# Two hybrid blocks on one core: the row-tiled matmuls of three mixers put on the full 128-row array

## The chip, the cores and the metric

The kernel runs on one core of one Trainium2 chip. TensorE (PE, with its weight loads listed as PEld), VectorE (DVE), ScalarE (ACT), GpSimd (POOL) and the DMA queue of SyncE (SP) work side by side. The metric is the device time of one execution in microseconds (us), as the median of the runs of a kernel.

## The reference

The reference is a first block and a second block on 512 grid tokens of 1024 features (the first block also reads 256 context tokens). Three places matter here.

The first block's mixer has an mLSTM with four heads, keys and queries 64 wide, values 128 wide. Per chunk, and in both directions of time, the output adds what the chunk's own scores give and what the carried state gives:

```
qk  = einsum('bhtd,bhsd->bhts', qb, kb) * w
num = einsum('bhts,bhse->bhte', qk, vb) + inter_w[..., None] * einsum('bhtd,bhde->bhte', qb, c_mem)
den = sum(qk, axis=-1) + inter_w * einsum('bhtd,bhd->bht', qb, n_mem)
h_out = num / maximum(abs(den), exp(-m_t))[..., None]
```

The second block has sparse attention: 16 heads of 64 in two groups, with three branches. A query of the selected branch sees its four best blocks of 64 keys, of the window branch its own window; both are masked softmaxes over scores q k^T. The second block also has a state-space mixer (32 heads of 64, chunks of 128), in which a decay `exp(acum[t] - acum[s])` of each head multiplies the scores of its group.

## The kernel before, in words

Activations lie feature-major, 128 features on the partitions and tokens along the free axis. Projections are done in three passes of fp32r matmuls over a high part and a low part of both operands (`mm3`, L210 to L212; L552 to L554 token-major). A matmul of fp32 operands shows as two instructions in the trace, one of fp32r as one.

A matmul whose operands lie on all 128 partitions uses the whole array; the profile writes it as 128*128 (rows*columns). One whose operands lie on 64 or 8 partitions is issued to a tile of 64 or 32 rows, written 64*128 or 8*128; one that writes 64 output partitions to a tile of 64 columns, 128*64.

The order of the work on every engine is set by a scheduler that plays the program on a timeline of its own (`schedule_with_timeline_sim=True`), led by priorities in program order; `later(n)` lets a piece yield. So a change of one instruction can move others. PSUM has eight banks, by use: `pa`, `pb` and `pf`; sparse attention has three banks of each of `pa` and `pb`, and two of `pf`.

The places that are touched:

- **mLSTM** (`ml_scan`). `iw` holds the query weights. L791 spreads them, L794 multiplies them into `qs` (4 multiplies of 128x512). Then, for each of four heads, L804 makes scores, L811 spreads maxima, L815 to L821 make the weights `wt` on DVE and ACT, and for each of four chunks and two directions L826 multiplies the weights with the values (128 rows) and L827 adds the queries times the carried state `cst`, 64 rows: the partitions of that head. Projections of the output gate (L552 to L554) fill gaps.
- **Sparse attention** (`nsa_step`). There are 64 steps: eight pairs of heads, four chunks `c` of queries, two heads of a pair. Each makes the scores of two branches `b` over `n = (c+1)*128` keys in a `pb` bank: L1399 takes the queries `q` (the head's high part on its own 64 partitions and its low part on the other 64) times the high part of the keys `kh`, which stands on both halves; L1400 adds the high part of the queries times the low part of the keys `kl`, 64 rows; for b = 0 and c of 2 or 3, L1402 adds the selection (`selT` times `cselr`, 8 rows); L1403 adds the causal mask on the last 128 columns. DVE takes the maximum (L1404), ACT the exponentials (L1406), which frees the bank; PE then transposes the weights (L1424) and multiplies them with the values (L1444, 128*64). Projections of z, in bank `pf`, fill gaps.
- **State-space mixer** (`ssd_group`). L1731 spreads a head's running decay over 128 partitions (`selr` times `acr`, 64 rows: 32 heads' high and low parts), L1751 does it for two heads at a time with `prs`.

```
nc.tensor.matmul(ps[:, :n], q[:, cc], kh[:, :n], start=True, stop=False)
nc.tensor.matmul(ps[:, :n], q[rows, cc], kl[rows, :n], start=False, stop=False)
if b == 0 and c >= 2:
    nc.tensor.matmul(ps[:, :n], E["selT"][g][:, c - 2, :], E["cselr"][:, :n], start=False, stop=False)
nc.tensor.matmul(ps[:, c * 128:n], E["idr"], E["cmr"], start=False, stop=True)
```

Of the kernel before, what the change touches and what calls it, by code (L numbers as in the profile page):

```python
# [10 lines left out]
F32 = mybir.dt.float32  # L11
F32R = mybir.dt.float32r
# [4 lines left out]
OP = mybir.AluOpType  # L17
AX = mybir.AxisListType
PSUM = bass.MemoryType.PSUM
# [21 lines left out]
class Kern:  # L41
# [6 lines left out]
    def banks(self, stage):  # L48
        """the eight banks of PSUM, by use, from here on"""
        pa, pb, pf = PS[stage]  # L50
        assert pa + pb + pf == 8
        if PS[max(stage - 1, 0)] == PS[stage] and stage:
            return
        self.psx.close()
        self.ps = self.psx.enter_context(self.tc.tile_pool(name="ps", bufs=1, space=PSUM, reuse_waits="tile"))
        self.psb = {"pa": pa, "pb": pb, "pf": pf}
# [13 lines left out]
    @contextmanager  # L70
    def later(self, n):
        """what is issued here yields to the next n instructions"""
        p = self.tc.cur_priority
        self.tc.cur_priority = p + n
        yield
        self.tc.cur_priority -= n
# [13 lines left out]
    def tmpf(self, name="tmpf"):  # L90
        """for work that fills gaps: not in line with the rest"""
# [28 lines left out]
    def lower_bounds(self, l0, l1, vec):  # L120
        """softmax over two rows of logits, first entry (columns [128, 8])"""
# [12 lines left out]
        # log(1 - lb)  # L134
# [4 lines left out]
    def columns(self, name, items, tag="pa"):  # L139
        """items: (key, ap of n*128 contiguous values, n); gives columns [128, n] of each."""  # L140
# [19 lines left out]
    def to_T(self, dst, src, ntok):  # L160
        """src DRAM [ntok,1024] -> dst [128, 8, ntok]"""
# [36 lines left out]
    def cols(self, w, c0, n):  # L198
        """columns c0..c0+n of w [K, N] as [128, K/128, n]"""
# [3 lines left out]
    def wrows(self, w, r0, nb):  # L203
        """row blocks r0.. (128 each) of w [K, N] as [128, nb, N]"""
# [9 lines left out]
    mvp = None      # pool of the rows' own room  # L214
# [4 lines left out]
    def silu_cols(self, aps, name):  # L219
        """columns of silu(c): [128, 8, len(aps)]"""  # L220
# [30 lines left out]
    def matvec(self, dst, w, sc, n, c0, nb, bias, tag=None):  # L251
        """dst [128, nb, n] = columns c0.. (nb blocks of 128) of silu(c) @ w + bias (bias [128, nb])"""
# [31 lines left out]
    def sumsq(self, x, n, tag, w2=None):  # L284
        """sums over the features of x^2 and, if asked for, of w2 x^2 [128 (all rows the same), n] in PSUM; x [128, 8, n]"""
# [20 lines left out]
    def table(self, name):  # L306
        """the activation table that comes next, after what has been issued"""
# [12 lines left out]
    def rstd(self, p, n, dim, name="rstd", dst=None, both=False, then=None):  # L320
        """1/sqrt(p/dim + eps) from PSUM p [128, n]; both: with the table that has both functions; then: the next table"""
# [7 lines left out]
    def halves(self, x, A, B):  # L329
        """the parts of norm_split for the grid's tokens, by half"""  # L330
        return [(x[:, :, t:t + 256], 256, A, B, t) for t in (0, 256)]

    def stats(self, parts):
        """1/rms of each of parts [(x, n, ..)]"""
# [4 lines left out]
    def norm_split(self, batches, hi, lo, rs=None):  # L339
        """batches: [[(x, n, A, B, t0)]]: hi + lo[:, :, t0:t0 + n] = x * rstd * A + B"""  # L340
# [21 lines left out]
    def ffn(self, w1, w2, hi, lo, segs, ends, begin=None, fill=()):  # L362
        """segs: [(t0, n, x, gate)]: x += gate * swiglu(hi + lo); gate already holds the half.
        ends: the segments for the first and last products, smaller for what waits and comes next"""
# [58 lines left out]
def constants():  # L423
# [29 lines left out]
    k["k_csel"] = (np.arange(512)[None, :] // 64 == np.arange(8)[:, None]).astype(f)  # L453
# [24 lines left out]
FB = (1, 1, 2)     # matrix-vector products beside a head of the mLSTM, of the HGRN, beside its last head  # L478
# [8 lines left out]
class Mix1:  # L487
    """HGRN2 and mLSTM over the context (256 tokens) and the grid (512 tokens)."""

    def mix1(self, i, hi, lo, vec, mrg, early):  # L490
        """hi, lo: [128, 8, 768] (grid tokens 0..511, context 512..767); mrg: DRAM [8, 128, 512]"""
# [36 lines left out]
    # one 128-column block, feature-major: fn(psum [128, n], t0, n)  # L528
# [11 lines left out]
    # token-major, 256 columns: fn(psum [128, 256], chunk)  # L540
# [16 lines left out]
    def wtok(self, w, c0):  # L557
        """256 columns of w, as two halves over k"""
# [10 lines left out]
    # ---------------------------------------------------------------- mLSTM  # L569
    def ml_project(self, i, w, vec):  # L570
# [10 lines left out]
        # q (chunks 0, 1: grid only) and k (chunks 2, 3), padded for the convolutions  # L581
# [3 lines left out]
        for ch in (2, 3, 0, 1):  # L585
# [15 lines left out]
            if ch == 3:  # L601
                # by half of the grid: the second one's norm comes later
# [8 lines left out]
        # v, token-major, with a column of ones  # L611
# [40 lines left out]
    def ml_scan(self, i, w, vec):  # L652
        nc, ml = self.nc, self.ml
        R = 56                                   # rows (dir, chunk, head): 0..23 forward, 32..55 backward
        # token-major gates, then rows
# [14 lines left out]
        row = lambda n: ml.tile([128, 128], F32, name=n)[:R]  # L670
        I, F = pr_[:R, 0:128], row("F")
        nc.vector.tensor_copy(F, pr_[:R, 128:256])
        # log sigmoid(f) = min(f, 0) - log1p(exp(-|f|))
# [8 lines left out]
        # cumulative sums and maxima within the chunks  # L682
# [6 lines left out]
        # the maximum carried from chunk to chunk  # L689
# [7 lines left out]
        ch = ml.tile([1, 4, 64], F32, name="ch")     # sum, maximum, carried m, carry weight  # L697
# [14 lines left out]
        mm = ml.tile([128, 2], F32, name="mmc")[:R]  # carried m, last maximum  # L712
# [5 lines left out]
        cwp = ml.tile([128, 2, 16], F32, name="cwp")  # [dir, (chunk, pair)]  # L718
# [3 lines left out]
        sw, iw, mt = (row(n) for n in ("sw", "iw", "mt"))  # L722
# [13 lines left out]
        # states  # L736
# [13 lines left out]
        for c in (4, 5, 0, 1, 2, 3):  # L750
# [13 lines left out]
            if c == 5:  # L764
                # context states -> first grid chunk of each direction
# [17 lines left out]
        # queries scaled for the states  # L783
        qs = ml.tile([128, 4, L], F32, name="qs")
        for pr in range(2):
            for d in range(2):
# [7 lines left out]
                nc.vector.tensor_mul(qs[:, pr * 2 + d, :], self.qT[:, pr, :], p)  # L794
        # scores, outputs
        self.hml = ml.tile([128, 4, 4, 128], F32, name="hml")
        ss = ml.tile([128, 4, 4], F32, name="mss")
        for h in range(4):
# [22 lines left out]
            for c in range(4):  # L821
                po = self.pt("pb")
                for d in range(2):
# [3 lines left out]
                    nc.tensor.matmul(o, qs[rows, pd, c * 128:(c + 1) * 128], cst[rows, pd, c, :], start=False, stop=True)  # L827
# [38 lines left out]
    # ---------------------------------------------------------------- HGRN2  # L866
# [8 lines left out]
    def hg_front(self, i, w, vec, h):  # L875
        """the projections of a head and what follows from them alone"""
# [12 lines left out]
        # of each direction: the sums of the log decays, B, and A = B + log k (backward) or B - log k (forward)  # L889
# [3 lines left out]
        for d in range(2):  # L893
# [32 lines left out]
            # the keys themselves, both directions added  # L926
# [9 lines left out]
    def hg_back(self, vec, h, mrg, front):  # L936
# [3 lines left out]
        # pairs at every level  # L940
# [6 lines left out]
        for d in range(2):  # L947
            B, A, Tt = BA[:, 1 + d, :L], BA[:, 3 * d, :L], Ta[:, d, :8]
            X, Y = BA[:, 2 * d, :L], BA[:, 2 * d + 1, :L]   # what the first and the second halves take
            sq, sk = (1, 0) if d == 0 else (0, 1)      # which half holds the queries / the keys  # L950
# [46 lines left out]
            # states between the chunks  # L997
# [3 lines left out]
            # U: from the chunk's start, V: to its end; queries and keys or keys and queries  # L1001
# [20 lines left out]
            # context  # L1022
# [15 lines left out]
            # transposed keys  # L1038
# [24 lines left out]
        # scores of both directions in one [key, query] tile  # L1063
# [19 lines left out]
        # norm over the head, gate  # L1083
# [11 lines left out]
        else:  # L1095
            # nothing reads the grid's rows any more
# [22 lines left out]
class Mix2:  # L1119
    LAT = [(0, 512)]  # L1120

    # ------------------------------------------------------------- rope tables
    def rope_tables(self, i, pool, cosd, sind):
        """cos and sin of the positions' angles, [128, 512], to DRAM"""
# [1417 lines left out]
```

## Time and profile before

| what | value |
|---|---|
| median of 3 runs | 2950.13 us (2944.2 to 2953.55) |
| span of the profiled execution | 2933.2 us |
| median less that span | 16.9 us |
| instructions | 41489 |
| PE busy | 2799.7 us, 95% (16545 matmuls) |
| PEld busy | 2114.3 us, 72% |
| DVE busy | 1548.8 us, 53% |
| ACT busy | 1000.1 us, 34% |
| POOL busy | 257.3 us, 9% |
| DMA | 373.95 MB, 40% of 16 engines' span |

The span is the time from the first to the last instruction of the profiled execution; the execution's own device time is not listed apart from the runs, so what lies around the span is taken as the 16.9 us between it and the median (11.0 to 20.4 us with the lowest and highest run). Times in a timeline count from the start of the span. A matmul's duration includes its pipeline, so two matmuls in a row overlap in the list; the time that one costs is the distance from its start to the next start.

### The profile page before, as it was taken

To read this page: it belongs to the slowest core of one execution; us is meant where nothing else is said; L and a number is where in the kernel's file an instruction comes from. 1 tells how busy PE (TensorE), PEld (TensorE's weight loads), DVE (VectorE), ACT (ScalarE), POOL (GpSimd) and SP (SyncE) were. 2 spreads that over 40 slices of the span, in tenths; PEclk is the share of its full clock that TensorE was granted. 3 is DMA by queue.
4 is the path that set the end of the run, shared out by engine and by line. 5 is a ranking of instruction groups with operands and counts; after the bars stand their busy time and mean duration, and the time that the engine had idled before them with its cause. 6 is when DMAs were issued, how large, how long until landed. Compare 5 with 4: busy or idle time off the path is not lost. (4 is left out here: it accounts for less than half of the span.)

```text
span 2933.2 us, 41489 instructions
## 1 busy us (share of the span) xinstructions
PE 2799.7 (95%) x16545; PEld 2114.3 (72%) x16546; DVE 1548.8 (53%) x3002; ACT 1000.1 (34%) x1793; POOL 257.3 (9%) x301
## 2 busy tenths in 40 slices
PE   7999999999998889999998999999999999989997
PEld 5788888889786666688887777666777768855553
DVE  6333333357358995543436556655666654543334
ACT  5211112144236663322224334444444533311112
POOL 2000000002001211000001000111222120000000
PEclk9999999999999899999999999999999999999999
DMA  7422122142512348533334332101233466378885
GB/s 259 139 87 79 51 65 65 59 129 72 151 52 65 85 155 284 170 94 98 95 90 142 95 92 74 30 12 45 80 101 104 131 204 203 110 272 280 289 305 186
DMA packets 386997, 373.95 MB, mean 127 GB/s; under 512 B 20321, under 2 KB 316645, under 8 KB 386546
## 3 DMA queue, kind: packets, MB, share of 16 engines
q1 hardware_dynamic: 386802, 371.28, 40.3%
q8 instruction: 131, 2.15, 0.3%
q14 instruction: 64, 0.52, 0.1%
HBM read 343.70 MB, written 27.53 MB: 127 GB/s over the span
## 5 line engine op out<-in xcount | busy, mean ns | idle before, releaser
L191 ACT CAST whi<-wraw 128x1024 fp32r<-128x1024 f32 x277 | 285.8, 1042 | 758.9 <-PE pppa L211 340.0
L210 PE MATMUL pppa<-lath,whi 128*128 128x512 f32 (+4 forms) x1344 | 521.9, 389 | 15.0 <-ACT whi L191 6.0
L211 PE MATMUL pppa<-latl,whi 128*128 128x512 f32 (+3 forms) x1344 | 519.9, 387 | 4.7 <-DVE latl L358 3.5
L212 PE MATMUL pppa<-lath,wlo 128*128 128x512 f32 (+3 forms) x1344 | 515.2, 385 | 0.5 <-DVE wlo L192 0.5
L192 DVE TENSOR_TENSOR wlo<-wraw,whi 128x1024 fp32r<-128x1024 f32 (+1 forms) x273 | 330.8, 1218 | 255.0 <-ACT whi L191 245.5
L210 PEld LDWEIGHTS pppa<-lath,whi 128*128 128x128 f32 (+3 forms) x1344 | 252.5, 188 | 81.1 <-ACT whi L191 12.9
L211 PEld LDWEIGHTS pppa<-latl,whi 128*128 128x128 f32 (+2 forms) x1344 | 252.2, 188 | 67.6 <-DVE latl L358 5.0
L212 PEld LDWEIGHTS pppa<-lath,wlo 128*128 128x128 f32 (+2 forms) x1344 | 252.1, 188 | 58.3 <-issue 4.5
L211 PE MATMUL pppb<-hl,whi 128*128 128x512 f32 (+1 forms) x576 | 195.4, 341 | 0.0
L210 PE MATMUL pppb<-hh,whi 128*128 128x512 f32 (+1 forms) x576 | 193.1, 344 | 0.0
L212 PE MATMUL pppb<-hh,wlo 128*128 128x512 f32 (+1 forms) x576 | 191.6, 341 | 0.0
L416 DVE SCALAR_TENSOR_TENSOR xT<-pppb,sG,xT 128x512 f32<-128x512 f32 (+1 forms) x144 | 96.8, 690 | 135.0 <-PE pppb L212 134.8
L396 DVE TENSOR_TENSOR hf<-sg,pppa 128x256 f32<-128x256 f32 (+1 forms) x68 | 39.7, 584 | 232.5 <-PE pppa L212 232.0
L210 PE MATMUL pppf<-lath,whi 128*128 128x512 f32 x320 | 129.7, 405 | 7.9 <-ACT lath L1823 2.9
L2109 PE MATMUL pppa<-ew,xg 128*64 128x512 f32 x512 | 131.2, 597 | 0.0
L210 PE MATMUL pppa<-ctxh,whi 128*128 128x256 f32 (+1 forms) x440 | 124.1, 282 | 5.4 <-DVE W L912 5.1
L212 PE MATMUL pppf<-lath,wlo 128*128 128x512 f32 x320 | 127.8, 400 | 0.6 <-DVE wlo L192 0.6
L211 PE MATMUL pppf<-latl,whi 128*128 128x512 f32 x320 | 128.0, 400 | 0.0
L210 PEld LDWEIGHTS pppb<-hh,whi 128*128 128x128 f32 x576 | 108.0, 188 | 27.3 <-issue 5.8
L212 PE MATMUL pppa<-ctxh,wlo 128*128 128x256 f32 (+1 forms) x440 | 124.2, 282 | 0.0
L211 PE MATMUL pppa<-ctxl,whi 128*128 128x256 f32 (+1 forms) x440 | 123.8, 281 | 0.3 <-POOL ctxl L356 0.3
L211 PEld LDWEIGHTS pppb<-hl,whi 128*128 128x128 f32 x576 | 108.4, 188 | 16.1 <-issue 3.4
(698 smaller groups left out, 5195.5 us busy)
## 6 DMA issues: line engine op xcount, KB each, us to landing
wraw<-in_ffn_w_dram SPq DMA_DIRECT2D x132, 512.0 KB, 4.0
wraw<-in_w_in_dram SPq DMA_DIRECT2D x102, 512.0 KB, 4.2
ew<-in_w_exp_gate_dram SPq DMA_DIRECT2D x64, 512.0 KB, 9.6
ew<-in_w_exp_up_dram SPq DMA_DIRECT2D x64, 512.0 KB, 8.7
ew<-in_w_exp_down_dram SPq DMA_DIRECT2D x32, 1024.0 KB, 11.2
mraw<-in_w_mod_dram SPq DMA_DIRECT2D x40, 512.0 KB, 7.0
wraw<-in_w_mod_dram SPq DMA_DIRECT2D x32, 512.0 KB, 4.3
mraw<-in_w_ada_dram SPq DMA_DIRECT2D x32, 512.0 KB, 7.0
```

The source lines that it names most:

```text
L191: nc.scalar.copy(hi[:, :n], raw[:, :n])
L192: (nc.gpsimd if pool else nc.vector).tensor_sub(lo[:, :n], raw[:, :n], hi[:, :n].bitcast(F32))
L210: nc.tensor.matmul(out, wh, xh, start=start, stop=False)
L211: nc.tensor.matmul(out, wh, xl, start=False, stop=False)
L212: nc.tensor.matmul(out, wl, xh, start=False, stop=stop)
L396: nc.vector.tensor_mul(h[:, :n], sg[:, :n], pp[1])
L416: nc.vector.scalar_tensor_tensor(x[:, o, :], p[:, :n], gate[:, o:o + 1], x[:, o, :], op0=OP.mult, op1=OP.add)
L2109: nc.tensor.matmul(ph[x * 64:x * 64 + 64, :], xg[:, k, pr * 128 + x * 64:pr * 128 + x * 64 + 64], wts[k // 4 * 2 + x][:, k % 4, :], start= ...
```

## The change

L827, L1400, L1402, L1731 and L1751 are issued over all 128 rows; L791, L804 and L811 (64 and 56 rows) stay as they are:

- mLSTM: `qs` gets a second axis for the two heads of a pair. The half of the partitions that is the other head's is zeroed by two memsets on POOL, and L794's four multiplies of 128 partitions become eight of 64. The state matmul then reads all of `qs` and `cst`. To make room, `sw`, `iw` and `mt` take the buffers of `e`, `w1` and `dd`.
- Sparse attention: the low-part matmul reads all 128 partitions of `q` and `kl`. Both halves of `kl` are already the same, so the low part of the queries times the low part of the keys is added as well. `selT` and `cselr` become 128 rows; the constant is 128x512 with zero rows, `selT` is zeroed on DVE before its first 8 rows are written, once for each of two groups.
- State-space mixer: `selr`, `prs` and `acr` become 128 rows; the lower 64 of `acr` are zeroed once on DVE.

```diff
-    k["k_csel"] = (np.arange(512)[None, :] // 64 == np.arange(8)[:, None]).astype(f)
+    cs = np.zeros((128, 512), f)
+    cs[:8] = np.arange(512)[None, :] // 64 == np.arange(8)[:, None]
+    k["k_csel"] = cs
...
-        sw, iw, mt = (row(n) for n in ("sw", "iw", "mt"))
+        sw, iw, mt = (row(n, tag) for n, tag in (("sw", "e"), ("iw", "w1"), ("mt", "dd")))
...
-        qs = ml.tile([128, 4, L], F32, name="qs")
+        qs = ml.tile([128, 4, 2, L], F32, name="qs")
+        for q in range(2):
+            nc.gpsimd.memset(qs[64 - q * 64:128 - q * 64, :, q, :], 0.0)
...
-                nc.vector.tensor_mul(qs[:, pr * 2 + d, :], self.qT[:, pr, :], p)
+                for q in range(2):
+                    r = slice(q * 64, q * 64 + 64)
+                    nc.vector.tensor_mul(qs[r, pr * 2 + d, q, :], self.qT[r, pr, :], p[r, :])
...
-                    nc.tensor.matmul(o, qs[rows, pd, c * 128:(c + 1) * 128], cst[rows, pd, c, :], start=False, stop=True)
+                    nc.tensor.matmul(o, qs[:, pd, h % 2, c * 128:(c + 1) * 128], cst[:, pd, c, :], start=False, stop=True)
...
-            cselr = na.tile([8, 512], F32R, name="cselr")
+            cselr = na.tile([128, 512], F32R, name="cselr")
             t = self.tmp("csel")
-            nc.sync.dma_start(t[:8, :], i["k_csel"])
-            nc.vector.tensor_copy(cselr, t[:8, :])
+            nc.sync.dma_start(t, i["k_csel"])
+            nc.vector.tensor_copy(cselr, t)
...
+                nc.vector.tensor_scalar(selT, self.ident[:, None, :].to_broadcast([128, 2, 128]), 0.0, None, op0=OP.mult)
...
-            nc.tensor.matmul(ps[:, :n], q[rows, cc], kl[rows, :n], start=False, stop=False)
+            nc.tensor.matmul(ps[:, :n], q[:, cc], kl[:, :n], start=False, stop=False)
...
-            acr = sd.tile([64, L], F32R, name="acr")
+            acr = sd.tile([128, L], F32R, name="acr")
+            nc.vector.tensor_scalar(acr[64:128], self.sel4[64:128, 0:1].to_broadcast([64, L]), 0.0, None, op0=OP.mult)
...
-                nc.tensor.matmul(p, selr[:, r:r + 1].to_broadcast([64, 128]), acr, start=True, stop=True)
+                nc.tensor.matmul(p, selr[:, r:r + 1].to_broadcast([128, 128]), acr, start=True, stop=True)
```

The diff also drops comments and adds lines, so that line numbers shift (L827 becomes L833, L1400 becomes L1407, L1731 becomes L1740).

The number of matmuls stays 14076 in the program. What moves is their order in the mLSTM and in the linear-attention heads behind it (HGRN), since the scheduler plays another program. In the sparse attention's steps the PE rows stand in the same order as before.

PE, at the start of the mLSTM's heads (`qT,kT` are the scores of L804, `M,ident` the spread maxima of L811, `whi,lath` and the like the output gate's projections). Before:

```order
L791 MATMUL pppb<-iw,ident 64x128 x32
L804 MATMUL pppb<-qT,kT 128x128 x4
L811 MATMUL pppb<-M,ident 128x128 x4
L552 MATMUL pppa<-whi,lath 128x256
L553 MATMUL pppa<-wlo,lath 128x256
L811 MATMUL pppb<-M,ident 128x128 x4
L554 MATMUL pppa<-whi,latl 128x256
```

The same place in the changed program:

```order
L795 MATMUL pppb<-iw,ident 64x128 x32
L554 MATMUL pppa<-whi,lath 128x256
L555 MATMUL pppa<-wlo,lath 128x256
L556 MATMUL pppa<-whi,latl 128x256
L810 MATMUL pppb<-qT,kT 128x128 x4
L554 MATMUL pppa<-whi,lath 128x256
L555 MATMUL pppa<-wlo,lath 128x256
L817 MATMUL pppb<-M,ident 128x128 x4
```

Five projections now stand ahead of the first spread maxima, where there were none; six more, no longer shown, stand before the second four, where there were two.

ACT, between the first and the second HGRN head (L908 and L914 are the logarithms of the next head's gates, L973 and L979 exponentials of the current one; an ACT_TABLE_LOAD stands where the function changes). Before:

```order
L908 ACT_TABLE_LOAD
L908 ACTIVATE W<-W,tiny 128x2x768
L928 ACT_TABLE_LOAD
L928 ACTIVATE ks<-W,lno 128x512
L1085 ACTIVATE hsq<-pppb 128x512
L1010 ACTIVATE fq<-BA 128x4x64
L1019 ACTIVATE eT<-T_8755 128x4
L1011 ACTIVATE fq<-fq 128x4x64
L312 ACT_TABLE_LOAD
L312 ACTIVATE rstdl<-pppb,eps 128x512
L973 ACT_TABLE_LOAD
```

The same place in the changed program:

```order
L934 ACT_TABLE_LOAD
L934 ACTIVATE ks<-W,lno 128x512
L1025 ACTIVATE eT<-T_8761 128x4
L911 ACTIVATE W<-W 128x1536
L979 ACTIVATE z<-z 128x512 x6
L1016 ACTIVATE fq<-BA 128x4x64
L1023 ACTIVATE fk<-fk 128x512
L1091 ACTIVATE hsq<-pppb 128x512
L891 ACTIVATE g<-pppa 128x512
L914 ACT_TABLE_LOAD
L914 ACTIVATE W<-W,tiny 128x2x768
L312 ACTIVATE rstdl<-pppb,eps 128x512
```

The norm's logarithm (L312) now stands with the gates' logarithm behind one table load; over all heads ACT has two table loads fewer.

## Rows read from the trace of the kernel before

**Rows 1.** Busy time by engine in stretches (start:end length, busy, clock, DMA).
```profile
core 0: us, PE busy (x) PEld busy (x) DVE busy (x) ACT busy (x) POOL busy (x), PEclk, DMA share, GB/s
1727.00:2022.00 295.00, 292.45 (x1725) 200.93 (x1725) 172.90 (x474) 127.79 (x365) 45.08 (x66) 0.99 0.14 41
...
796.00:802.00 6.00, 6.00 (x86) 5.61 (x82) 6.00 (x12) 2.42 (x4) 0.00 (x0) 1.00 0.80 227
802.00:809.00 7.00, 6.72 (x32) 6.29 (x32) 4.76 (x13) 1.26 (x2) 0.00 (x0) 0.56 0.36 95
...
800.00:870.00 70.00, 69.72 (x444) 59.76 (x444) 37.96 (x123) 23.30 (x73) 0.00 (x0) 0.95 0.17 47
870.00:1130.00 260.00, 225.46 (x2637) 177.40 (x2636) 216.40 (x452) 152.68 (x242) 45.80 (x56) 0.93 0.39 118
```

**Rows 2.** PE timeline (start us, duration us), sparse attention: 512, 256, 128 keys.
```profile
1900.17 0.47 PE L1399 MATMUL pppb<-kh,qs 128*128 128x512 f32 x1
1900.57 0.50 PE L1400 MATMUL pppb<-kl,qs 64*128 64x512 f32 x1
1901.00 0.49 PE L1402 MATMUL pppb<-cselr,selT 8*128 8x512 f32 x1
1901.42 0.33 PE L1403 MATMUL pppb<-cmr,idr 128*128 128x128 f32 x1
1901.59 0.33 PE L1399 MATMUL pppb<-kh,qs 128*128 128x256 f32 x1
1901.85 0.38 PE L1400 MATMUL pppb<-kl,qs 64*128 64x256 f32 x1
1902.16 0.33 PE L1403 MATMUL pppb<-cmr,idr 128*128 128x128 f32 x1
...
1909.62 0.32 PE L1400 MATMUL pppb<-kl,qs 64*128 64x128 f32 x1
1909.87 0.33 PE L1403 MATMUL pppb<-cmr,idr 128*128 128x128 f32 x1
```

**Rows 3.** PE timeline: first and last of a full-array stream, 256 and 512 columns.
```profile
821.10 0.28 PE L554 MATMUL pppa<-whi,latl 128*128 128x256 f32 x1
...
825.37 0.28 PE L554 MATMUL pppa<-whi,latl 128*128 128x256 f32 x1
...
2118.98 0.40 PE L212 MATMUL pppf<-lath,wlo 128*128 128x512 f32 x1
...
2123.88 0.39 PE L212 MATMUL pppf<-lath,wlo 128*128 128x512 f32 x1
```

**Rows 4.** The line of the low-part matmul: counts, durations ns, and its shapes.
```profile
L1400 PE MATMUL pppb<-kl,qs x128: 322/434/576, 1727.1 to 2012.9; 64*128 64x256 f32 x32, 64*128 64x128 f32 x32, 64*128 64x384 f32 x32, 64*128 64x512 f32 x32
```

**Rows 5.** Waits from 1727 to 2022 us (waiter, releaser, us, times, longest).
```profile
PEld pppb L1402 <- issue: 6.9, 32, 0.2
...
PEld pppb L1399 <- ACT P L1406: 3.9, 11, 0.8
```

**Rows 6.** PE timeline, mLSTM: first of three pairs, and what follows; the line's counts.
```profile
829.17 0.49 PE L826 MATMUL pppb<-vml,wt 128*128 128x129 f32 x2
...
831.67 0.39 PE L552 MATMUL pppa<-whi,lath 128*128 128x256 f32 x1
...
L827 PE MATMUL pppb<-cst,qs x64: 271/272/374, 809.6 to 864.3; 64*128 64x129 f32 x64
```

**Rows 7.** PE timeline, HGRN: first and ninth of nine full-array fp32 pairs.
```profile
942.31 0.39 PE L1080 MATMUL pppb<-P,vhg 128*128 128x128 f32 x2
...
944.09 0.39 PE L1082 MATMUL pppb<-fq,st 128*128 128x128 f32 x2
```

**Rows 8.** The line of the spread decay, and an idle time before it (us, times).
```profile
L1731 PE MATMUL pppb<-acr,selr x32: 383/492/625, 2078.8 to 2373.0; 64*128 64x512 f32 x32
...
  DVE st L1713: 6.1, 11
```

**Rows 9.** The query multiplies on DVE (busy us, mean ns).
```profile
L794 DVE TENSOR_TENSOR qs<-qT,pppb 128x512 f32<-128x512 f32 x4 | 2.7, 683 | 0.0
```

**Rows 10.** Full-array weight loads of the projections (busy us, mean ns).
```profile
L210 PEld LDWEIGHTS pppa<-lath,whi 128*128 128x128 f32 (+3 forms) x1344 | 252.5, 188 | 81.1 <-ACT whi L191 12.9
```

More of the change, by code (lines that the diff above doesn't have):

```diff
@@ L669, in ml_scan @@
             nc.tensor.transpose(pr_[:R, ty * 128:(ty + 1) * 128], gp[:, ty, :], self.ident)
-        row = lambda n: ml.tile([128, 128], F32, name=n)[:R]
+        row = lambda n, tag=None: ml.tile([128, 128], F32, name=n, tag=tag or n)[:R]
         I, F = pr_[:R, 0:128], row("F")
@@ L1334, in select @@
                         op=OP.mult)
-                selT = nb.tile([8, 2, 128], F32R, name="selT", bufs=2)
+                selT = nb.tile([128, 2, 128], F32R, name="selT", bufs=2)
                 iv = imp[:, 2:4, :]
@@ L1353, in select @@
                     nc.tensor.transpose(pst[:8, c * 128:(c + 1) * 128], rk[:, c, :], self.ident)
-                nc.vector.tensor_copy(selT, pst[:8, :256].rearrange("p (c t) -> p c t", c=2))
+                nc.vector.tensor_copy(selT[:8], pst[:8, :256].rearrange("p (c t) -> p c t", c=2))
                 pcT = nb.tile([128, 2, L], F32, name="pcT", bufs=2)
@@ L1391, in nsa_step @@
         q = E["qs"][hp, par]
-        rows = slice(par * 64, par * 64 + 64)
         cc = slice(c * 128, (c + 1) * 128)
@@ L1562, in ssd @@
             nc.sync.dma_start(tri, i["k_tri128"])
-            selr = sd.tile([64, 32], F32R, name="selr")
-            nc.vector.tensor_copy(selr, self.sel4[:64, :])
+            selr = sd.tile([128, 32], F32R, name="selr")
+            nc.vector.tensor_copy(selr, self.sel4)
             small = sd.tile([32, 3], F32, name="dsm")
@@ L1719, in ssd_group @@
         sq = None
-        prs = sd.tile([64, 4, 128], F32R, name="prs", bufs=1)
-        nc.vector.tensor_copy(prs.rearrange("p j (q d) -> p (j q) d", q=2), selr[:, hs][:, :, None].to_broadcast([64, 8, 64]))
+        prs = sd.tile([128, 4, 128], F32R, name="prs", bufs=1)
+        nc.vector.tensor_copy(prs.rearrange("p j (q d) -> p (j q) d", q=2), selr[:, hs][:, :, None].to_broadcast([128, 8, 64]))
         for j in range(4):
```

## The prediction

> **What bounds the kernel now.** I read the busy time by stretch first. In sparse attention, 1727 to 2022 us, PE is busy for 292.45 of 295 us, DVE for 172.9, ACT for 127.8 [rows 1]: PE sets the pace. In the mLSTM's heads, 800 to 870 us, PE is busy for 69.72 of 70 us and DVE for 38 [rows 1]. In the HGRN heads behind them, to 1130 us, DVE is the fuller one, 216 of 260 us [rows 1].
>
> But a busy PE need not be a PE at its peak, so the second view is the timeline, read by distances between starts. In sparse attention a 512-column matmul over 128 rows is followed by the 64-row one after 0.40 us, that by the 8-row one after 0.43 us, that by the mask, over 128 rows again, after 0.42 us [rows 2]. The same width on the full array, row after row, takes (2123.88 - 2118.98) / 21 = 0.233 us (22 rows from the first to the last) [rows 3]. So each change between the full array and a row tile costs nearly 0.2 us in which PE starts nothing, though it counts as busy. The load engine's view says it too: before the 8-row matmul it stood idle 32 times for 6.9 us together, 0.22 us each, with nothing to wait for ("issue") [rows 5]. At 256 columns the distances are 0.26 and 0.31 us [rows 2], against (825.37 - 821.10) / 36 = 0.119 us in a full-array stream (37 rows) [rows 3].
>
> **The change, part by part.** The sum is made against the profiled span of 2933.2 us; the median lies 16.9 us above it, which I leave as it is.
>
> *Sparse attention.* The low-part matmul runs 32 times at each of four widths [rows 4], the selection 16 times at each of the two larger, 32 in all [rows 5]. On the full array I take 0.233 us at 512 columns and 0.119 at 256 [rows 3]; 0.17 at 128, which the mask, itself 128 columns over 128 rows, takes to the next start (1901.42 to 1901.59) [rows 2]; for 384 no row here, so the mean of its neighbours. Going in saves 0.40 - 0.233 = 0.17 us at 512, 0.26 - 0.119 = 0.14 at 256, at 384 their mean 0.155, and at 128 what coming out saves, 0.25 - 0.17 = 0.08: 32 x 0.545 = 17.4 us. Coming out of the low part saves 0.20, 0.195, 0.19 and 0.08 us: 32 x 0.665 = 21.3 us. Coming out of the selection saves 0.19 and 0.195 us: 16 x 0.385 = 6.2 us. Together 45 us of PE's time. What is late next is the chain behind each score bank: maximum on DVE, exponential on ACT, bank free. Today PE's loads wait for that only 11 times, 3.9 us [rows 5]; with 250 us of PE left, DVE would be at 173 / 250 = 69%. I take 40 us, allowing 5 us for such waits; the ends are 28 us (some 17 us of new waits) and 45 us.
>
> *mLSTM.* Three pairs of L826 and L827 take 831.67 - 829.17 = 2.50 us, 0.83 us a pair, that is for four instructions [rows 6]. The HGRN's output makes just such sums wholly on the full array: eight distances of two instructions in 944.09 - 942.31 = 1.78 us, 0.111 us an instruction [rows 7], so 0.445 us for four. There are 64 L827 instructions [rows 6], so 32 pairs: 32 x (0.83 - 0.445) = 12 us at most, since some stand two and two already. The weights `wt` are made on DVE and ACT between the groups, and DVE has room there [rows 1]. I take 9 us, ends 0 and 12.
>
> *State-space mixer.* 32 matmuls of L1731 [rows 8] and, by the code, 16 of L1751. With 0.2 us each way they cost at most 48 x 0.2 = 9.6 us, if two changes are shared by neighbours; but PE waits for DVE's states before L1731 anyway, 6.1 us [rows 8], and the next is often a column tile (L1741), where a change remains. I take 2 us, ends 0 and 10.
>
> *What is added.* L794 becomes eight multiplies of 64 partitions. Their columns stay, and a row of 128x512 took 683 ns [rows 9], so I reckon 4 x 0.68 = 2.7 us more on DVE, which from 796 to 802 us is busy all 6 us [rows 1]. The first states are needed only behind some twenty projections, which the new order keeps ahead of them, so I put it at nothing; without that cover it costs 2.7 us. The two memsets go to POOL, idle throughout 800 to 870 us [rows 1]; `selT` and `acr` are zeroed on DVE in three operations of no more columns than a multiply in rows 9, so at most 2 us, off PE's path. The selection's constant is read once, as 128 rows instead of 8, ahead of its stage. The reused buffers of the mLSTM's rows hold values whose last readers stand before: no new wait. Each nothing; if all covers fail, 5 us.
>
> *What moves.* PE's and ACT's order in the mLSTM and the HGRN heads is new, 330 us in all. ACT loses two table loads, but DVE is the fuller engine there. I see no direction: nothing, within 6 us either way.
>
> Sum: 40 + 9 + 2 = 51 us, a span of 2882 us and a median of 2950 - 51 = **2899 us**. The span's ends are -19 us (28, less 3 for the multiplies and 6 for the order) and -73 us (45 + 12 + 10 + 6), so 2931 and 2877 us.
>
> **Rivals.**
>
> *The consumers become the bound (0.18).* DVE's and ACT's queues are in order, and the steps' maxima, exponentials and copies share them; if PE waits for banks for 20 us more, sparse attention gives 20 to 25 us, all together some 33 us: 2917 us. For it: three banks for scores, and waits on ACT already there [rows 5]. Against it: 69% is not full, and the projections of z need neither.
>
> *Full-array loads don't hide, no gain (0.03).* If a weight load over all rows had to wait for the running matmul, a low-part matmul of 256 columns would start 0.119 + 0.188 = 0.31 us after its predecessor (0.188 us is such a load's duration [rows 10]), as late as today, and the time would stay at 2950 us. The streams speak against it: a new load before each matmul, and 0.119 us from start to start [rows 3], less than one load. The Trainium skill's page "TensorE: Matmul & The Clock Gate" says in Part 3, "The mechanism", that a weight load overlaps running matmuls only when the row group differs; by that rule the 64-row tiles would be the better form and this rival would hold. The trace's streams don't agree with it.
>
> *The clock falls, slower (0.03).* From 802 to 809 us PE had a granted clock of 0.56, mostly the lower level of 1.2 GHz, right after a stretch of row and column tiles (L791, L804, L811) [rows 1]. In sparse attention it has 0.99 [rows 1]. Should shorter work and new waits bring it down there, the 250 us left would stretch to 250 / 0.85 = 294 us at a mean clock of 0.85: from there the gain is gone, and at 0.75 (333 us) the kernel would be at about 2977 us, with 11 us gained elsewhere. Against it: the change takes tiles out, and the full-array streams run at the full clock.
>
> *All of it, and a better order (0.08).* Each term at its upper end and a few us from the two table loads: about 2880 us.
>
> **How the numbers follow.** The forecast has 0.68. Of the cases, forecast, bounded consumers and the full gain are faster by over 0.3% (8.9 us, about what a measurement of this kernel can tell from no change): 0.94. No gain is 0.03, slower 0.03. The range for 8 in 10 reaches from the full gain, 2880 us, to a little past bounded consumers with a worse order, 2924 us.
>
> **What would show it.** In the changed profile, distances at L1407 and L1409 of about 0.23 us at 512 columns and 0.12 at 256; no idle "issue" time of loads before them; four instructions of L832 and L833 in 0.45 us; sparse attention some 255 us long, with PE still nearly full. If the distances fall but the stage stays over 270 us with PE idle for banks, the consumers were the bound. If the distances stay, the price was not that of the row tile. If the stretch from 800 to 1130 us changes by more than 15 us, the order was the larger part, and my sum is wrong there.

## The result, and the profile after

The changed kernel takes 2877.96 us (median of 4 runs, 2875.16 to 2881.13) against 2947.16 us for the kernel before in the same comparison (median of 4, 2936.67 to 2953.55): a ratio of 0.9767, 95% interval 0.9743 to 0.979. It is faster, as forecast, but by 69 us where the forecast had 51, and 2 us below the lower end of the stated range.

The profiled execution of the changed kernel has a span of 2873.4 us in a run of 2875.16 us. So 1.8 us lie around a span, not 16.9. In the traces below, L826 is now L832, L1399, L1402 and L1403 are L1406, L1409 and L1410, L1406 is L1413, L1424 is L1431, L1444 is L1451, L804 is L810 and L811 is L817.

Where the 59.8 us between the two spans lie, read from the ends of the same instructions in both timelines (us from the start of the span):

| place | before | after | difference |
|---|---|---|---|
| last spread of the query weights (L791, now L795) | 799.8 | 802.1 | +2.3 |
| last state matmul of the mLSTM (L827, now L833) | 864.6 | 858.0 | -6.6 |
| gated output of HGRN heads 1 to 4 | 961.7, 1023.8, 1077.5, 1134.8 | 961.1, 1014.9, 1068.8, 1135.7 | -0.6, -8.9, -8.7, +0.9 |
| first mask matmul of sparse attention | 1727.8 | 1726.4 | -1.4 |
| last mask matmul of sparse attention | 2014.1 | 1960.7 | -53.4 |
| state-space mixer, last head | 2389.6 | 2328.6 | -61.0 |
| end of the span | 2933.2 | 2873.4 | -59.8 |

Sparse attention, from first to last mask, went from 286.3 to 234.3 us: 52.0 us of the 59.8. The mLSTM's part, from the spread to the last state matmul, went from 64.8 to 56.0 us, and what it won is gone at the end of the HGRN heads. The state-space mixer, from the last mask to its last head, went from 375.5 to 367.9 us. The busy time by stretch of the changed kernel, to be held against [rows 1]:

```profile
core 0: us, PE busy (x) PEld busy (x) DVE busy (x) ACT busy (x) POOL busy (x), PEclk, DMA share, GB/s
1726.00:1961.00 235.00, 231.45 (x1645) 183.03 (x1643) 166.40 (x463) 124.78 (x360) 43.21 (x62) 1.00 0.18 51
802.00:809.00 7.00, 5.73 (x30) 4.81 (x28) 6.82 (x12) 0.14 (x1) 0.00 (x0) 0.71 0.53 132
800.00:870.00 70.00, 68.32 (x511) 63.27 (x507) 50.32 (x147) 27.17 (x78) 2.39 (x1) 0.93 0.23 62
870.00:1130.00 260.00, 222.96 (x2626) 175.73 (x2624) 208.06 (x437) 146.25 (x236) 45.81 (x55) 0.93 0.40 121
```

PE is still full in sparse attention, 231 of 235 us, with DVE at 166: the engine that sets the pace has not changed, its work has become shorter. The timeline of the new scores shows how (start, duration; compare with [rows 2]):

```profile
1868.39 0.50 PE L1406 MATMUL pppb<-kh,qs 128*128 128x512 f32 x1
1868.73 0.40 PE L1407 MATMUL pppb<-kl,qs 128*128 128x512 f32 x1
1868.97 0.22 PE L1410 MATMUL pppb<-cmr,idr 128*128 128x128 f32 x1
1869.03 0.28 PE L1431 MATMUL pppa<-ident,P 128*128 128x128 f32 x1
1869.06 0.48 PE L1406 MATMUL pppb<-kh,qs 128*128 128x512 f32 x1
1869.37 0.39 PE L1407 MATMUL pppb<-kl,qs 128*128 128x512 f32 x1
1869.60 0.39 PE L1409 MATMUL pppb<-cselr,selT 128*128 128x512 f32 x1
1869.83 0.22 PE L1410 MATMUL pppb<-cmr,idr 128*128 128x128 f32 x1
1869.98 0.33 PE L1451 MATMUL pppa<-PT,vt 128*64 128x128 f32 x2
```

L1407 to L1409 and L1409 to L1410 are 0.23 us now, as forecast. The mask is what was not forecast: it is followed after 0.06 us (1868.97 to 1869.03), where before it took 0.17 [rows 2]. And L1406, right behind a value matmul on a column tile (L1451, 128*64), still takes 0.34 us at 512 columns (1868.39 to 1868.73), 0.1 more than in a stream [rows 3]; behind a transpose (L1431) it takes 0.31 (1869.06 to 1869.37). The waits for score banks grew, but little. PE's own, before and after, and the load engine's after ([rows 5] had 3.9 us in 11):

```profile
PE pppb L1399 <- ACT P L1406: 1.9, 5, 0.6
```

```profile
PEld pppb L1406 <- ACT P L1413: 7.3, 21, 1.2
...
PE pppb L1406 <- ACT P L1413: 3.4, 8, 1.0
```

In the mLSTM the pairs of [rows 6] became a stream, four instructions in 0.44 us (815.29 to 815.73), as forecast:

```profile
815.29 0.39 PE L833 MATMUL pppb<-cst,qs 128*128 128x129 f32 x2
815.51 0.39 PE L832 MATMUL pppb<-vml,wt 128*128 128x129 f32 x2
815.73 0.39 PE L833 MATMUL pppb<-cst,qs 128*128 128x129 f32 x2
```

### The profile page after: what moved, and what is told of

It is laid out like the page before. It is cut to its first block, busy times and chain, and to the rows that moved or that the text cites. A ratio compares the mean times of both kernels' runs of the same rounds, so it can differ in the third digit from the quotient of the medians.

```text
span 2873.4 us, 41502 instructions
## 1 busy us (share of the span) xinstructions
PE 2731.4 (95%) x16545; PEld 2099.0 (73%) x16546; DVE 1551.9 (54%) x3009; ACT 996.1 (35%) x1791; POOL 264.2 (9%) x303
```

## The experiments

Each of the ten kernels was run beside the kernel before on the same chip; the changed kernel was not run again beside them, and three chips were used (the kernel before had medians of 2941 to 2948 us on them). "Stage" is sparse attention from first to last mask matmul in the trace.

| kernel | median us | ratio to before, 95% interval | stage us |
|---|---|---|---|
| sparse attention's edits alone | 2883.88 | 0.9796 (0.9753 to 0.984) | 234.4 |
| mLSTM's edit alone | 2944.92 | 1.0004 (0.9978 to 1.0029) | 292.1 |
| state-space mixer's edit alone | 2941.0 | 0.9984 (0.9963 to 1.0005) | 296.2 |
| before, low part issued twice | 2956.6 | 1.0039 (1.0022 to 1.0057) | 304.6 |
| low part's edit alone | 2899.04 | 0.983 (0.9786 to 0.9873) | 247.6 |
| the change without the mLSTM's edit | 2878.63 | 0.9762 (0.9719 to 0.9805) | 234.4 |
| changed, mLSTM's spreads on 128 rows too | 2876.91 | 0.9758 (0.9715 to 0.98) | 234.4 |
| changed, early work yields to 280 | 2879.99 | 0.9769 (0.9723 to 0.9814) | 234.3 |
| changed, values one pair later | 2865.5 | 0.9753 (0.9722 to 0.9785) | 225.7 |
| spreads on 128 rows and values later | 2862.86 | 0.9744 (0.9701 to 0.9787) | 225.7 |

### One part of the change at a time

Sparse attention alone:

```diff
-nc.tensor.matmul(ps[:, :n], q[rows, cc], kl[rows, :n], start=False, stop=False)
+nc.tensor.matmul(ps[:, :n], q[:, cc], kl[:, :n], start=False, stop=False)
...
-selT = nb.tile([8, 2, 128], F32R, name="selT", bufs=2)
+selT = nb.tile([128, 2, 128], F32R, name="selT", bufs=2)
...
```

> The kernel before with sparse attention's two edits alone (low-part matmul on 128 rows, selection on 128 rows). In the changed kernel that stage is 52 us shorter (287.0 to 234.5 us), where the prediction had 40 and at most 45. Theory A: all of the 52 us belong to these two edits, since a change to a row tile also delays the matmul behind the change: stage of 234 to 236 us, about 2895 us in all. Theory B: 45 us is the edits' worth and the rest came in from the other stages' new order (work of the neighbours that runs elsewhere now): stage of 241 to 243 us, about 2902 us.

The stage took 234.4 us: theory A. All 52 us belong to these two edits. But the time fell to 2883.9 us, 62 us below the 2945.85 us of the runs beside it and 11 below what theory A gave. Between the two profiled spans the difference is 50.4 us (2933.2 to 2882.8). The other ten or so are in the runs of the kernel before, not in the edit; the next two kernels, in which sparse attention is untouched, point to where.

The mLSTM alone, and the state-space mixer alone (`acr`, `prs` and the selection of decays on 128 rows):

```diff
-nc.tensor.matmul(o, qs[rows, pd, c * 128:(c + 1) * 128], cst[rows, pd, c, :], start=False, stop=True)
+nc.tensor.matmul(o, qs[:, pd, h % 2, c * 128:(c + 1) * 128], cst[:, pd, c, :], start=False, stop=True)
...
```

> The kernel before with the mLSTM's edit alone. Theory A: the last state matmul of the mLSTM comes about 9 us earlier, and the HGRN heads behind it give it all back, because their order of instructions is new: HGRN's end within 3 us of before, about 2947 us in all (no change). Theory B: the 9 us are kept, and something else in the changed kernel took them: HGRN's end 7 to 10 us earlier, about 2938 us.

```diff
-selr[:, r:r + 1].to_broadcast([64, 128]), acr
+selr[:, r:r + 1].to_broadcast([128, 128]), acr
...
```

> The kernel before with the state-space mixer's edit alone. Theory A (its price as in sparse attention, two changes and a late matmul each for 31 changes fewer): 6 to 8 us less in the state-space mixer's stage, about 2940 us. Theory B (the prediction's): 2 us less, since PE waits for DVE's states there anyway, about 2945 us.

The mLSTM's last state matmul came 7.4 us earlier, and the last HGRN head's gated output 3.5 us later (1138.3 against 1134.8 us): theory A, no gain in the time. The state-space mixer, from the last mask to its last head, took 372.7 us against 375.5 in the kernel before: 3 us, nearer theory B. The changed kernel's own profile had 367.9 us there, 7.6 less, but in that execution the granted clock was at its lower level for 6.8 us of the stage, against 17.1 in the kernel before. Over all profiles of this study it is 371.3 us on average in the seven kernels with the new form (367.9 to 373.0, with 7 to 17 us of low clock) and 376.1 in the five with the old (375.0 to 378.1, with 17 to 24). At the same 17.1 us of low clock it is 375.5 us in the kernel before and 372.4 and 373.0 in two kernels with the new form, some 3 us less. Whether the new form also shortens the low stretches is not shown.

In both kernels, the untouched sparse attention was longer than in the kernel before, 292.1 and 296.2 against 286.3 us, by the same instructions. Busy times by stretch of the state-space mixer's kernel, and of the mLSTM's:

```profile
1950.00:1960.00 10.00, 10.00 (x27) 5.05 (x26) 3.53 (x11) 3.16 (x10) 1.33 (x2) 0.50 0.00 1
1960.00:1970.00 10.00, 10.00 (x28) 6.01 (x28) 3.89 (x11) 3.06 (x10) 0.77 (x1) 0.50 0.01 2
```

```profile
1950.00:1960.00 10.00, 10.00 (x39) 5.56 (x35) 4.90 (x14) 4.31 (x14) 1.33 (x2) 0.73 0.00 0
1960.00:1970.00 10.00, 10.00 (x42) 7.09 (x42) 3.74 (x10) 2.38 (x8) 1.80 (x2) 0.50 0.01 2
```

The granted clock is 0.50, the lower level of 1.2 GHz, for some 27 us in all in the one (from 1946 us on) and some 17 in the other, with PE busy throughout. In the profiled execution of the kernel before it fell too, for some 3 us from 1874 us on:

```profile
1870.00:1876.00 6.00, 5.38 (x25) 3.43 (x26) 4.30 (x11) 3.41 (x9) 0.77 (x1) 0.88 0.00 0
1876.00:1882.00 6.00, 5.78 (x43) 4.64 (x41) 2.99 (x10) 1.82 (x6) 1.58 (x2) 0.83 0.01 3
```

In the eight profiles with the new low part (the changed kernel's and those of seven experiments) it is 1.00 through the whole stage. The runs say the same without a profile: in the 43 runs of the kernel before beside the experiments the time follows the mean granted clock, from 2927.8 us at 0.981 to 2957.1 us at 0.969 (median 2946.0). So the runs of the kernel before differ by up to 30 us with the clock, and part of that lies in this stage.

### Does the small tile cost, or the change of tile?

The kernel before, with the low part issued twice in a row:

```diff
 nc.tensor.matmul(ps[:, :n], q[rows, cc], kl[rows, :n], start=False, stop=False)
+nc.tensor.matmul(ps[:, :n], q[rows, cc], kl[rows, :n], start=False, stop=False)
```

> The kernel before with each of the 128 low-part matmuls of sparse attention issued twice, one behind the other, both on 64 rows (the low part is added twice, so the output is not the reference's there). Theory A (the change of tile costs, not the small tile): the second one starts after the pitch of a full-array matmul, 0.233 us at 512 columns, 0.175 at 384, 0.118 at 256 and 0.06 to 0.11 at 128; 32 x 0.59 to 32 x 0.63 = 19 to 20 us more, about 2967 us. Theory B (a 64-row matmul is itself slow): each costs as much as the first, 0.42, 0.37, 0.31 and 0.25 us to the next start: 32 x 1.35 = 43 us more, about 2990 us. Theory C (a second one is hidden behind the drain): less than 8 us more.

The timeline, with L1400 and L1401 as the pair:

```profile
1905.55 0.48 PE L1399 MATMUL pppb<-kh,qs 128*128 128x512 f32 x1
1905.96 0.50 PE L1400 MATMUL pppb<-kl,qs 64*128 64x512 f32 x1
1906.30 0.39 PE L1401 MATMUL pppb<-kl,qs 64*128 64x512 f32 x1
1906.62 0.33 PE L1404 MATMUL pppb<-cmr,idr 128*128 128x128 f32 x1
```

The second does not start after 0.233 us but after 0.34; the mask behind it, though, comes after 0.32 us instead of 0.43. The pair takes 0.66 us where one took 0.43 [rows 2]: the second adds 0.23 us, the price of a full-array matmul. By the medians over all of them it adds 0.231, 0.181, 0.12 and 0.113 us at 512, 384, 256 and 128 columns, 32 x 0.645 = 20.6 us; the stage, at a clock of 1.00, took 304.6 us, 18.3 us more than in the profile of before, or about 20 without what the clock cost there. The time is only 10.7 us above the 2945.85 us of the runs beside it, not 21, since those runs lose more to the clock: its ten runs have a mean clock of 0.976 to 0.981, theirs 0.970 to 0.981. Theory A holds in its sum: a 64-row tile is no slower than the full array, the change is. Its detail was wrong in an instructive way: a change costs twice, about 0.1 us for the matmul in front of it and 0.1 us for the first one behind it, whatever their form. That is why the mask, first behind a change, took 0.17 us [rows 2] and now takes 0.06 in front of a full-array matmul.

The low part's edit alone, which leaves 32 lone selections on 8 rows:

```diff
-nc.tensor.matmul(ps[:, :n], q[rows, cc], kl[rows, :n], start=False, stop=False)
+nc.tensor.matmul(ps[:, :n], q[:, cc], kl[:, :n], start=False, stop=False)
```

> The kernel before with the low-part edit of sparse attention alone; the 32 selection matmuls stay on 8 rows, each now a lone tile between full-array matmuls. Theory A (the price is per change of tile, about 0.09 us before the tile, 0.19 us behind it and 0.10 us at the mask that follows): 96 low parts without a selection give back all three, 35.7 us together, the 32 with one only one change each, 32 x 0.19 = 6 us: the stage is 42 us shorter than before, about 247 us long. Theory B (the price is per small matmul): the stage is only 32 x 0.19 = 6 us longer than in the kernel with both edits, about 241 us long.

```profile
1879.97 0.48 PE L1399 MATMUL pppb<-kh,qs 128*128 128x512 f32 x1
1880.28 0.40 PE L1400 MATMUL pppb<-kl,qs 128*128 128x512 f32 x1
1880.61 0.49 PE L1402 MATMUL pppb<-cselr,selT 8*128 8x512 f32 x1
1881.03 0.33 PE L1403 MATMUL pppb<-cmr,idr 128*128 128x128 f32 x1
```

The stage took 247.6 us, 13.3 us more than with both edits: theory A (247), not B (241). A lone 8-row matmul costs 13.3 / 32 = 0.42 us over the full array: 0.33 and 0.42 us to the next starts instead of 0.23, and the late mask. Before, the same matmul stood behind another row tile and cost only the one change more.

### Where the mLSTM's gain went

The change without the mLSTM's edit, that is with its lines as they were before, this one above all:

```diff
-nc.tensor.matmul(o, qs[:, pd, h % 2, c * 128:(c + 1) * 128], cst[:, pd, c, :], start=False, stop=True)
+nc.tensor.matmul(o, qs[rows, pd, c * 128:(c + 1) * 128], cst[rows, pd, c, :], start=False, stop=True)
...
```

> The changed kernel without the mLSTM's edit (sparse attention and state-space mixer alone). Theory A (the mLSTM's gain is lost in the last HGRN head, so its edit is worth nothing): 2876 to 2881 us, that is the 2883.9 us of sparse attention's edits alone less 3 to 8 us for the state-space mixer, the same as the changed kernel's 2878 us within 4 us. Theory B (the mLSTM's edit is worth its 9 us): 2885 us or more. For the state-space mixer: 3 us less than in the kernel before (as when it was changed alone) or 8 to 10 us less (as it stands in the changed kernel).

2878.63 us against 2877.96, ratios of 0.9762 and 0.9767: theory A, the mLSTM's edit is worth nothing that can be measured. In the profiles, from the last spread to the first mask of sparse attention, 924.3 us pass in the changed kernel, 927.0 with the edit alone, and 928.1 and 925.2 in the eighth and ninth experiments, which have the edit in the same form: 926.2 on average. In the six without it they are 926.2 to 929.4, on average 928.2 (928.0 before). So of 9 us some 2 arrive, within the spread of the profiles.

The changed kernel with its mLSTM's two spreads on 128 rows too:

```diff
-self.ident[:R, r:r + 1].to_broadcast([R, 128]), M,
+self.ident[:, r:r + 1].to_broadcast([128, 128]), Mf,
...
+nc.gpsimd.memset(Mf, 0.0)
...
```

> The changed kernel with the mLSTM's two spreads (L810 and L817, on 56 rows) also on 128 rows, the rows from 56 on zero. Theory A (changes of tile and the low clock behind them are the price here too): the matmuls of L817 start 0.11 us apart without the 0.2 us at either side, the mLSTM's last state matmul comes 3 to 6 us earlier than in the changed kernel. Theory B (DVE, which scales the queries, sets the pace there): less than 1 us. In all at most 6 us, since the HGRN heads may give it back: 2872 to 2880 us.

```profile
802.00:809.00 7.00, 7.00 (x60) 6.74 (x59) 6.79 (x12) 0.39 (x1) 0.00 (x0) 1.00 0.61 157
800.00:870.00 70.00, 66.98 (x526) 62.38 (x522) 45.60 (x139) 25.01 (x75) 2.41 (x1) 1.00 0.22 61
```

The low clock between 802 and 809 us went (1.00, after 0.71 in the changed kernel and 0.56 before [rows 1]), and PE did 526 instead of 511 matmuls by 870 us. Yet the last state matmul came 4.2 us later, not 3 to 6 earlier, and the time, 2876.91 us, is the changed kernel's within its spread. Neither theory had that. The trace shows why: between the last spread of the query weights and the last state matmul PE now does 464 matmuls instead of 419. The 45 more are full-array projections of 512 columns, 45 x 0.233 = 10.5 us by the price of [rows 3], and the stretch grew by only 4.7 us (56.0 to 60.7). For the same work it is some 6 us shorter, and about 5 of them are the clock, which was low for 10.2 us of that stretch in the changed kernel and for none here. It was low for none of it in the state-space mixer's kernel either, with the old spreads, so that the edit took the low clock away is not shown. From the last spread to the first mask of sparse attention it took 923.0 us, against 924.3 in the changed kernel.

One number of the changed kernel, how many instructions the early work beside the last HGRN head yields to:

```diff
-EARLY = 200
+EARLY = 280
```

> The changed kernel with one number changed: the work issued early beside the last HGRN head yields to 280 instructions instead of 200. In the changed kernel 27 matmuls of the output projection stand ahead of that head's last nine output matmuls, and PE then has nothing to do for 5 us of its normalisation (1131.4 to 1136.4 us); before, these projections stood behind the output and covered it. With 280 they stand behind it again. Theory A (lost cover is where the mLSTM's gain went): the last head's gated output comes 6 to 9 us earlier than in the changed kernel, about 1127 to 1130 us, and the time falls to 2869 to 2873 us. Theory B (the gain went elsewhere, DVE's work or the clock): less than 2 us, 2876 to 2879 us.

The stretch in question, in the changed kernel and then with 280:

```profile
1128.00:1132.00 4.00, 2.73 (x17) 1.70 (x15) 0.00 (x0) 2.33 (x3) 0.00 (x0) 1.00 0.47 116
1132.00:1136.00 4.00, 0.00 (x0) 0.00 (x0) 1.44 (x2) 2.43 (x4) 0.00 (x0) 0.57 0.95 313
1136.00:1140.00 4.00, 3.61 (x10) 2.90 (x11) 1.75 (x3) 0.98 (x2) 0.00 (x0) 0.57 1.03 376
```

```profile
1128.00:1132.00 4.00, 3.85 (x17) 2.77 (x15) 2.75 (x4) 2.43 (x4) 0.00 (x0) 1.00 0.93 242
1132.00:1136.00 4.00, 2.39 (x9) 1.53 (x9) 1.16 (x2) 1.32 (x2) 0.00 (x0) 1.00 1.00 325
1136.00:1140.00 4.00, 3.66 (x16) 2.99 (x17) 3.90 (x7) 2.06 (x4) 0.00 (x0) 1.00 1.00 349
```

The cover came back: PE no longer stands still from 1132 to 1136 us, and its clock no longer falls behind the pause. The gated output came at 1131.6 us, 4.1 earlier than in the changed kernel (6 to 9 were expected). The time did not move, 2879.99 us. The heads ahead of it were already 5.3 us earlier in this execution, so the last head, from the third gated output to the fourth, was no shorter, 68.1 against 66.9 us; and the 27 projection matmuls that had run ahead of the output, 27 x 0.233 = 6.3 us, now run behind it. So the pause is real and is where PE stood idle, but filling it moves the same work and wins nothing. What sets the length from the HGRN heads through the output projection I did not settle; the DMA engines are busy for 0.80 to 0.99 of the time from 1120 to 1200 us in both kernels, and no run here changed those transfers.

### A version that beats both

If the price per change holds for column tiles too, the 640 value matmuls (128*64) are next: they still stand scattered among full-array ones. Issuing them one pair of steps later takes 52 changes out of the program:

```diff
-VD = 0
+VD = 1
```

> The changed kernel with one number changed in sparse attention: the value matmuls (column tiles of 64, L1451) of a pair of steps are issued one pair later (VD 1 instead of 0), so that fewer of them stand alone among full-array matmuls; the program then has 52 changes of tile fewer, that is 26 round trips. Theory A (the price per round trip holds for column tiles too, about 0.4 us): 26 x 0.4 = 10 us less in the stage, 224 us instead of 234.3, about 2868 us in all. Theory B (the eight buffers of the transposed weights are then held longer, and PE waits for them): the stage is as long or longer, PE's waits for copies into PT grow, 2878 us or more.

```profile
1725.00:1951.00 226.00, 223.81 (x1644) 181.42 (x1642) 165.24 (x464) 122.49 (x359) 42.24 (x62) 1.00 0.18 52
```

The stage went from 234.3 to 225.7 us and the time to 2865.5 us (6 runs, 2864.22 to 2872.0): theory A, 8.6 / 26 = 0.33 us a round trip where 0.4 was expected. PE's own waits for score banks fell with it, from 3.4 to 1.6 us; without them the price is 6.9 / 26 = 0.26 us. The ratio to the kernel before, 0.9753, is not clear of the changed kernel's 0.9767, since their intervals overlap; what speaks for the gain is the stage in the traces, and that the six runs all lie below the changed kernel's four (2875.16 to 2881.13). With the mLSTM's spreads on 128 rows as well:

> The changed kernel with the mLSTM's two spreads on 128 rows (as in the seventh experiment) and the value matmuls one pair later (as in the ninth). Theory A: the two add up, 1 us and 10 us, about 2867 us. Theory B: what the ninth gives, since the mLSTM's part does not come out at the end.

2862.86 us (4 runs, 2860.01 to 2872.28), the lowest median here; from the last spread to the first mask it took 922.3 us, the shortest of all, but whether its last 3 us over the ninth are real its four runs don't tell.

## Why the prediction was right or wrong

**What bounds, and the direction: right.** PE bound sparse attention, the gaps were changes of tile, and taking them out left PE full for a shorter time.

**The mask's price: the step of the sum that failed.** "0.17 at 128, which the mask, itself 128 columns over 128 rows, takes to the next start" took that price from a row which itself stood right behind a row tile, so it held the very cost that was to be removed. The sum then gave nothing for the mask. Added up over the stage, the distances from each matmul to the next start were, in us:

| term | forecast | measured, before less after |
|---|---|---|
| into the low part (from L1399) | 17.4 | 38.98 - 27.72 = 11.3 |
| out of the low part (from L1400) | 21.3 | 43.35 - 20.52 = 22.8 |
| out of the selection (from L1402) | 6.2 | 12.63 - 6.58 = 6.1 |
| from the mask (L1403) to the next | 0 | 26.09 - 16.77 = 9.3 |
| new waits for banks | -5 | -1.5 by PE's waits, held in the row above |
| all other matmuls of the stage | 0 | 2.5 |

The measured rows make the 52.0 us, against 40. The mask's distance fell by 0.10 to 0.11 us in 84 of 127 cases (from 0.16 to 0.06 in front of a full-array matmul) and by 0.05 in 28; new waits, before the next high part, took some of that back (PE's 1.9 us became 3.4). The last row is in the main the clock's fall in the profile of before, some 1.7 us (half of 3.4). The term "into the low part" was too large by 6 us, because it set the high part's distance after the change to that of a stream, 0.233 us at 512 columns. It stayed at 0.34 behind a value matmul (7 of the 32) and at 0.31 behind a transpose (21 of them), and was 0.23 only behind projections (2). The first fits a change of tile; a transpose runs on the full array, and why the matmul behind it is late is not shown. So the three named terms gave 40 us where 45 were reckoned, the 5 us taken off for waits were not needed in full, and the mask's 9.3 us, waits included, came on top: the upper end of 45 us was too low.

**"the median lies 16.9 us above it, which I leave as it is": wrong.** It was taken as time around the span. 1.8 us lie there; the other 15 were the difference between one execution and the median of three, and the runs tie it to the granted clock. The two profiled executions have the same mean clock, 0.980, and the same time at the lower level, 116.6 and 116.1 us, and between them the change is worth 59.8 us. The runs of one clock agree: at 0.981 the difference is 54 us, at 0.980 58, at 0.976 61 and at 0.975 64. So some 60 of the 69 us are the kernel's, where the sum had 51, and the other nine or so are clock that the kernel before lost in most of its runs. The rival "the clock falls" looked at the right quantity in the wrong kernel: it asked whether the change would bring the clock down, and it was in three of the four profiles of the old form that it fell in this stage.

**mLSTM: right in size, wrong in effect.** 9 us were forecast and 8.8 came (64.8 to 56.0 us); in profiles with the same 6.8 us of low clock in that stretch it was 64.8 to 65.3 us without the edit and 54.6 and 54.7 with it, 10 us. But "what moves" was put at nothing within 6 us either way, and from the last state matmul to the last gated output the changed kernel lost 7.5 us. The lost cover behind the last head is where PE stood idle, but bringing it back won nothing, so what took the gain stays open. It was luck for the number that this loss and the too small terms of sparse attention work against each other.

**State-space mixer: small, as said**, some 3 us at an equal clock for the 2 forecast, within its ends. **What is added: nearly right**, PE waits for the split query multiplies 0.77 us at the first scores and 0.50 at a spread of maxima, against 0.3 in all before.

**Rivals.** Consumers did not become the bound: PE's waits for banks grew by 1.5 us, DVE is at 166 of 235 us. Full-array loads do hide: a load for L1407 lasts 0.19 us, and at 128 columns the next matmul starts 0.112 us after L1407's. The rule cited for that rival, from the Trainium skill's page "TensorE: Matmul & The Clock Gate", Part 3, "The mechanism", is not borne out by these rows. Nor would it have favoured the 64-row form here: that tile's neighbours are full-array matmuls, whose rows take in its own. The Trainium skill's page "TensorEngine Tiling (Array Packing)" says under "Key Properties" that a change of tiling mode drains TensorE. The trace agrees as far as it goes: next to a change the next start comes about 0.1 us late on either side, 0.3 to 0.4 us for a round trip. That the array runs empty in that time, no row shows. "All of it, and a better order", 2880 us, was nearest in time, but its reason, each term at its upper end and two table loads fewer, is not what happened.

## What to carry to other kernels

Count changes of tile in the program order, not small matmuls: a row or column tile standing alone among full-array matmuls costs some 0.3 to 0.4 us a visit here, a row tile standing behind its like costs no more than a full-array matmul, so either pad it with zero rows or group it. Price an instruction from a row whose neighbours are those it will have after the change; a row next to the thing removed carries its cost. And before taking a profiled execution for the median, look at how the runs' granted clock goes with their time: here the runs of one kernel differ by up to 30 us with it.

## What was not expected of the hardware

A change of tile is paid on both sides: about 0.1 us at the matmul in front of it and 0.1 us at the first one behind, even when that one's form is already the engine's (L1401 behind L1400: 0.34 us, against 0.233 in a stream). A selection of 8 rows and a low part of 64 next to each other pay it too.

The granted clock fell to the lower level in the middle of sparse attention at no fixed place, with PE busy throughout: at 1874 us for some 3 us in the profile of before, behind a wait of 0.61 us for a bank; from 1946 us on for some 27 us in another kernel with the same stage, with no such wait ahead. In the kernel with the low part twice it stayed at 1.00 through the stage, and its ten runs lie within 8.6 us (2952.76 to 2961.33). So row tiles alone need not bring it down, and what does stays open.
